# Softmax times V on one core: dropping the waits of copies and exps on their own engine's preceding write of a buffer, and one copy per loop body moved from VectorE to ScalarE

## The chip, the cores and the metric

The kernel runs on one core of one Trainium2 chip. The metric is the device time of one execution in microseconds (us).

Five engines appear below: TensorE (PE in the profile, with PEld for its weight loads), VectorE (DVE), ScalarE (ACT), GpSimd (POOL), and SyncE (SP), which issues the transfers (DMA).

## The reference

```python
def reference(scores, v):          # scores 8x12x1024x1024, v 8x12x1024x64, float32
    scores_max = np.max(scores, axis=-1, keepdims=True)
    attn = np.exp(scores - scores_max)
    attn = attn / (np.sum(attn, axis=-1, keepdims=True) + 1e-8)
    return np.matmul(attn, v).astype(np.float32)
```

There are 96 heads. The scores are 403 MB, so each element is read once and everything else has to hide behind that read.

## The kernel before

A head's 1024 query rows lie as 8 rows of 128 (one per partition). Four heads form a loop body (24 bodies), so a body has 32 such rows. One row goes through these stages:

1. ScalarE takes the exp of the scores (two rows per instruction; one at a time for the last six rows of a body).
2. PE transposes the row in eight 128x128 pieces into a PSUM tile `psT`.
3. VectorE copies `psT` to an SBUF tile `pt` (four of each, used in turn).
4. PE multiplies `pt` with V and a column of ones in eight accumulating products, two rows later.
5. After four or eight rows VectorE takes the reciprocals of the sums and scales the result; SyncE stores it.

```python
    def finish(u):                      # two rows behind
        ...
        for c in range(C):              # C = 8
            nc.tensor.matmul(
                out=bank[:, g * M : (g + 1) * M],
                lhsT=pt[:, c * P : (c + 1) * P],
                rhs=st["vones"][:, c, 0:M],
                start=(c == 0),
                stop=(c == C - 1),
            )
        if k % 2 == 1:
            if g == G - 1 and (b > 0 or k < AHEAD - 1):
                normalise(k, st, b, b + 1)
        ...
    def heads(n0):
        for k in range(AHEAD):          # 4 heads
            for r in range(R):          # 8 rows
                ...                     # exp of one or two rows into p_nat (ScalarE)
                psT = take(psT_bufs)
                for c in range(C):
                    nc.tensor.transpose(
                        out=psT[:, c * P : (c + 1) * P],
                        in_=p_row[:, c // L, c % L, :],
                        identity=order16[:],
                    )
                pt = take(pt_bufs)
                copy = nc.vector.tensor_copy(out=pt[:], in_=psT[:])
                if k == AHEAD - 1 and r == R - 1:
                    normalise(k, st, 0, 1, copy)   # first half of the last head
                ...
                if len(pending) > LAG:             # LAG = 2
                    finish(pending.pop(0))
```

Nothing in the source says so, but in the compiled program every one of PE's instructions, each weight load and each matmul, adds 1 to PE's semaphore when it is done.

The softmax here doesn't subtract the row's maximum and nothing guards it: scores larger than these inputs give would overflow.

## Time and profile before

| | before |
|---|---|
| device time, median of 3 runs | 1063.8 us (1063.76 to 1064.1) |
| span of the profiled run | 1062.3 us |
| busy: PE, PEld, DVE, ACT | 722.0, 676.5, 679.9, 740.1 us |
| DMA in use at nine tenths or more | 39 of 40 slices, about 432 GB/s |
| last row of scores lands, its exp starts | 1052.02, 1052.27 us |
| last copy on VectorE starts | 1055.18 us |
| last scaling product ends, second store issued, landed | 1058.00, 1058.25, 1060.30 us |

Times of single events are from the start of the span. The page is read from the outside in: whether one resource is full over the whole span (it is the DMA), and where it stops being full (after 1050 us, the tail). This is PE's timeline for the same steady stretch (start, duration, engine, line, instructions in the group):

```profile
26.28 0.61 PE L267 MATMUL psT<-order,p_nat 128*128 128x128 f16 x8
...
26.98 0.61 PE L267 MATMUL psT<-order,p_nat 128*128 128x128 f16 x8
...
27.69 0.61 PE L267 MATMUL psT<-order,p_nat 128*128 128x128 f16 x8
```

The transposes of successive rows start 0.70 us apart, and end, by the trace, at 26.89, 27.59 and 28.30. So by these records PE delivers a row every 0.70 us, VectorE can copy one every 0.60 us, and yet a copy comes only every 0.96 us.

### The profile page before, as it was taken

To read this page: it belongs to the slowest core of one execution; us is meant where nothing else is said; L and a number is where in the kernel's file an instruction comes from. 1 tells how busy PE (TensorE), PEld (TensorE's weight loads), DVE (VectorE), ACT (ScalarE), POOL (GpSimd) and SP (SyncE) were. 2 spreads that over 40 slices of the span, in tenths; PEclk is the share of its full clock that TensorE was granted. 3 is DMA by queue.
4 is the path that set the end of the run, shared out by engine and by line. 5 is a ranking of instruction groups with operands and counts; after the bars stand their busy time and mean duration, and the time that the engine had idled before them with its cause. 6 is when DMAs were issued, how large, how long until landed. Compare 5 with 4: busy or idle time off the path is not lost.

```text
span 1062.3 us, 33094 instructions
## 1 busy us (share of the span) xinstructions
PE 722.0 (68%) x12288; PEld 676.5 (64%) x12288; DVE 679.9 (64%) x1205; ACT 740.1 (70%) x480; POOL 243.5 (23%) x406
## 2 busy tenths in 40 slices
PE   2765766767766767667576776767677686666776
PEld 2755756666655667666576666766566676665765
DVE  1765756757666666666676666767567576676667
ACT  3766776666767668676685866767666677666686
POOL 3113112131121311212112221132121311203113
PEclk9988888879898787887988878889888788899889
DMA  9999999999999999999999999999999999999996
GB/s 397 430 417 434 428 434 434 432 435 428 434 432 432 427 433 435 434 434 427 433 429 435 428 433 435 426 441 431 431 434 429 430 428 438 434 434 432 426 432 260
DMA packets 25059, 453.05 MB, mean 426 GB/s; under 512 B 2784, under 2 KB 2784, under 8 KB 9440
## 3 DMA queue, kind: packets, MB, share of 16 engines
q1 hardware_dynamic: 25056, 453.00, 99.4%
q8 instruction: 3, 0.05, 0.0%
HBM read 436.21 MB, written 25.17 MB: 434 GB/s over the span
## 4 chain that ended last, share of the span: by engine, by line
DMA 62%; PE 12%; PEld 6%; DVE 5%; ACT 5%; issue 3%; POOL 3%; SPq 1%; POOLq 1%; ACTq 0%; DVEq 0%; PEldq 0%
DMA s_nat<-in_scores_dram 62%; PE psT L267 7%; DVE pt L273 5%; ACT p_nat L255 5%; PE psO L146 3%; POOL vones L212 3%; PEld L267 3%; PEld L146 3%; PE psO_whole L146 1%; SPq L203 1%; SPq L191 0%; POOLq L212 0%; POOLq L229 0%; POOLq L293 0%; POOLq L321 0%
## 5 line engine op out<-in xcount | busy, mean ns | idle before, releaser
L255 ACT ACTIVATE p_nat<-s_nat 128x2048 f16<-128x2048 f32 (+1 forms) x456 | 709.4, 1630 | 219.1 <-DMA s_nat<-in_scores_dram 192.3
L267 PE MATMUL psT<-order,p_nat 128*128 128x128 f16 x6144 | 562.8, 246 | 281.3 <-ACT p_nat L255 280.9
L273 DVE COPY pt<-psT 128x1024 f16<-128x1024 f16 x768 | 518.1, 689 | 367.1 <-PE L146 134.9
L267 PEld LDWEIGHTS <-p_nat 128*128 128x128 f16 x6144 | 445.4, 123 | 303.5 <-ACT p_nat L255 300.8
L212 POOL CAST vones<-v_sb 32x512 f16<-32x512 f32 x400 | 242.8, 607 | 815.3 <-PE L267 440.3
L146 PEld LDWEIGHTS <-pt 128*128 128x128 f16 x6144 | 302.8, 106 | 76.1 <-DVE pt L273 72.0
L146 PE MATMUL psO<-vones,pt 128*128 128x65 f16 x3072 | 177.5, 202 | 41.4 <-DVE pt L273 39.8
L146 PE MATMUL psO_whole<-vones,pt 128*128 128x65 f16 x3072 | 189.7, 209 | 11.6 <-DVE pt L273 11.2
L255 ACT ACT_TABLE_LOAD x24 | 30.8, 1283 | 94.1 <-DMA s_nat<-in_scores_dram 77.4
L130 DVE TENSOR_TENSOR out_sb<-psO,recip 64x256 f32<-64x256 f32 x192 | 81.2, 423 | 6.1
L130 DVE TENSOR_TENSOR out_sb<-psO_whole,recip 64x512 f32<-64x512 f32 x96 | 66.0, 688 | 3.0
L123 DVE RECIPROCAL recip<-psO 128x4 f32<-128x4 f32 x96 | 16.8, 175 | 0.8
L123 DVE RECIPROCAL recip<-psO_whole 128x8 f32<-128x8 f32 x48 | 9.5, 197 | 0.0
L71 DVE MEMSET vones<- 128x16 f16 x4 | 0.2, 72 | 0.8 <-PEq L310 0.8
L62 DVE CAST order<-ident 128x128 f16<-128x128 f32 x1 | 0.2, 227 | 0.4 <-POOL ident masks.py:199 0.4
masks.py:199 POOL TENSOR_SCALAR_AFFINE_SELECT ident<-ident 128x128 f32<-128x128 f32 x1 | 0.3, 292 | 0.1
masks.py:197 POOL MEMSET ident<- 128x128 f32 x1 | 0.2, 204 | 0.3 <-POOLq L310 0.3
L310 POOL MEMSET const-float32-0.0<- 128x1 f32 x1 | 0.1, 98 | 0.3 <-issue 0.3
L310 POOL MEMSET const-bfloat16-1.0<- 128x1 bf16 x1 | 0.1, 100 | 0.0
L310 POOL MEMSET const-uint8-127<- 128x1 uint8 x1 | 0.1, 100 | 0.0
L310 POOL MEMSET const-float32-1.0<- 128x1 f32 x1 | 0.1, 98 | 0.0
## 6 DMA issues: line engine op xcount, KB each, us to landing
s_nat<-in_scores_dram SPq DMA_DIRECT2D x96, 4096.0 KB, 33.0
v_sb<-in_v_dram SPq DMA_DIRECT2D x24, 1024.0 KB, 19.0
out_dram<-out_sb SPq DMA_DIRECT2D x47, 512.0 KB, 27.7
s_nat<-in_scores_dram SPq DMA_DIRECT2D x2, 2048.0 KB, 32.6
s_nat<-in_scores_dram SPq DMA_DIRECT2D x1, 1536.0 KB, 32.2
s_nat<-in_scores_dram SPq DMA_DIRECT2D x3, 512.0 KB, 20.7
s_nat<-in_scores_dram SPq DMA_DIRECT2D x1, 1024.0 KB, 25.4
out_dram<-out_sb SPq DMA_DIRECT2D x2, 256.0 KB, 2.0
```

The source lines that it names most:

```text
L62: nc.vector.tensor_copy(out=order16[:].rearrange("p (t j) -> p t j", t=T), in_=ident32[:].rearrange("p (j t) -> p t j", t=T),)
L71: nc.vector.memset(vo[:, :, D : D + 2], 1.0)
L123: inverse = nc.vector.reciprocal(out=recip, in_=psO[:, :, :, D : D + 1])
L130: nc.vector.tensor_tensor(out=rows.rearrange("j (b g) d -> j b g d", g=G), in0=psO[part, :, :, 0:D], in1=recip[part].to_broadcast([W, last ...
L146: nc.tensor.matmul(out=bank[:, g * M : (g + 1) * M], lhsT=pt[:, c * P : (c + 1) * P], rhs=st["vones"][:, c, 0:M], start=(c == 0), stop=(c ...
L203: nc.sync.dma_start(out=v_sb[:].rearrange("x h s l d -> x (h s l d)"), in_=rows[bass.ds(n // AHEAD, 1)].rearrange("o x y -> (o x) y"),)
L212: nc.gpsimd.tensor_copy(out=vones_bufs[k][s * Q : (s + 1) * Q, :, 0:D].rearrange("i (h l) d -> i h l d", l=L), in_=v_sb[k * Q : (k + 1) * ...
L255: nc.scalar.activation(out=p_nat[:, g : g + rows, :].rearrange("p r (x v) -> p x r v", v=Q * L), in_=s_bufs[k][:, r + g : r + g + rows, :] ...
L267: nc.tensor.transpose(out=psT[:, c * P : (c + 1) * P], in_=p_row[:, c // L, c % L, :], identity=order16[:],)
L273: copy = nc.vector.tensor_copy(out=pt[:], in_=psT[:])
L310: nc = _bacc.Bacc("TRN2", target_bir_lowering=False, num_devices=1)
```

## The change

Its intent: a copy into `pt` and an exp into `p_nat` need not wait for the earlier write of the same buffer by the same engine, since PE, which reads the buffer in between, is waited for anyway. The change declares those dependencies away. And in each body the copy of the last head's seventh row (index 6) goes to ScalarE, so that VectorE has less in front of the last copy.

```diff
     stores = []
-
-    def apart(dma, other):
-        tc.declare_no_dep(
-            dma.ins, other.ins, across_iterations=True, reason="stores of two heads are disjoint"
-        )
+    writers = {}
+
+    def apart(a, b, reason="stores of two heads are disjoint"):
+        tc.declare_no_dep(a.ins, b.ins, across_iterations=True, reason=reason)
+
+    def rewrite(buf, op):
+        others = writers.setdefault(buf.name, [])
+        for other in others:
+            apart(op, other, "readers in between")
+            apart(other, op, "readers in between")
+        apart(op, op, "readers in between")
+        others.append(op)
 ...
-                        nc.scalar.activation(
+                        exp = nc.scalar.activation(
 ...
+                        rewrite(p_nat, exp)
 ...
                 pt = take(pt_bufs)
-                copy = nc.vector.tensor_copy(out=pt[:], in_=psT[:])
+                if k == AHEAD - 1 and r == R - 2:
+                    nc.scalar.copy(out=pt[:], in_=psT[:])
+                else:
+                    copy = nc.vector.tensor_copy(out=pt[:], in_=psT[:])
+                    rewrite(pt, copy)
```

## The prediction

> **What bounds the kernel now.** I read the page's 40 slices and its DMA part first, then the chain that ended last, then the groups, and last the timeline of VectorE (DVE) in a steady stretch and at the end. The slices and the DMA part:
>
> ```profile
> DMA  9999999999999999999999999999999999999996
> GB/s 397 430 417 434 428 434 434 432 435 428 434 432 432 427 433 435 434 434 427 433 429 435 428 433 435 426 441 431 431 434 429 430 428 438 434 434 432 426 432 260
> ...
> q1 hardware_dynamic: 25056, 453.00, 99.4%
> ...
> DMA 62%; PE 12%; PEld 6%; DVE 5%; ACT 5%; issue 3%; POOL 3%; SPq 1%; POOLq 1%; ACTq 0%; DVEq 0%; PEldq 0%
> ```
>
> In 39 of 40 slices the DMA engines are at nine tenths or more, at about 432 GB/s; only the last slice falls to six tenths and 260 GB/s. The one queue's packets take 99.4% of the 16 engines' span, and the chain that ended last is led by DMA with 62%. 453.0 MB at 432 GB/s are 1049 us of the span of 1062.3. So the kernel is a transfer of 1050 us with a tail behind it. The windows put an edge on the tail (DMA share and GB/s are the last two numbers of a row):
>
> ```profile
> 148.00:1020.00 872.00, 604.05 (x10232) 567.26 (x10232) 565.42 (x997) 615.68 (x400) 194.00 (x320) 0.85 1.00 432
> ...
> 1048.00:1050.00 2.00, 2.00 (x47) 1.90 (x44) 1.46 (x3) 1.55 (x2) 0.00 (x0) 1.00 0.73 297
> 1050.00:1052.00 2.00, 2.00 (x37) 1.65 (x34) 1.78 (x5) 2.00 (x3) 1.82 (x3) 1.00 0.20 82
> 1052.00:1054.00 2.00, 1.23 (x22) 0.87 (x21) 1.97 (x4) 1.30 (x2) 0.61 (x1) 1.00 0.53 217
> 1054.00:1056.00 2.00, 1.52 (x34) 1.27 (x33) 1.81 (x5) 0.00 (x0) 0.00 (x0) 1.00 0.11 45
> 1056.00:1058.00 2.00, 0.36 (x8) 0.23 (x8) 1.87 (x5) 0.00 (x0) 1.19 (x2) 1.00 0.00 0
> ```
>
> Over 872 us the DMA share is 1.00. After 1050 it collapses, and DVE, the third engine of a row after PE and PEld, is busy 1.8 to 1.97 of every 2 us until 1058. That is the only stretch in which DVE can set the time.
>
> The groups concerned:
>
> ```profile
> L255 ACT ACTIVATE p_nat<-s_nat 128x2048 f16<-128x2048 f32 (+1 forms) x456 | 709.4, 1630 | 219.1 <-DMA s_nat<-in_scores_dram 192.3
> ...
> L273 DVE COPY pt<-psT 128x1024 f16<-128x1024 f16 x768 | 518.1, 689 | 367.1 <-PE L146 134.9
> ```
>
> DVE's 768 copies are 689 ns each; DVE idles 367 us in front of them and the page says mostly for PE. The timeline says otherwise (start, duration, idle before):
>
> ```profile
> 27.36 0.69 DVE L273 COPY pt<-psT 128x1024 f16<-128x1024 f16 x1 [0.27 <-PE L267]
> 28.32 0.69 DVE L273 COPY pt<-psT 128x1024 f16<-128x1024 f16 x1 [0.27 <-PE L146]
> 29.28 0.69 DVE L273 COPY pt<-psT 128x1024 f16<-128x1024 f16 x1 [0.27 <-PE L146]
> ...
> 1052.54 2.48 DVE L273 COPY pt<-psT 128x1024 f16<-128x1024 f16 x4
> 1055.18 0.69 DVE L273 COPY pt<-psT 128x1024 f16<-128x1024 f16 x1 [0.16 <-PE L146]
> 1055.79 0.17 DVE L123 RECIPROCAL recip<-psO 128x4 f32<-128x4 f32 x1
> 1056.00 0.88 DVE L130 TENSOR_TENSOR out_sb<-psO,recip 64x256 f32<-64x256 f32 x2
> 1056.91 0.18 DVE L123 RECIPROCAL recip<-psO 128x4 f32<-128x4 f32 x1
> 1057.12 0.88 DVE L130 TENSOR_TENSOR out_sb<-psO,recip 64x256 f32<-64x256 f32 x2
> ```
>
> In the steady stretch copies come every 0.96 us with the same gap of 0.27 us, although PE's transposes for them end earlier (those for the copy at 28.32 end at 27.59, modelled). Four copies in a row at 1052.54 overlap and come every 0.60 us. So DVE itself loses 0.36 us on some copies. I sorted all 768 copies by their place in the loop body (32 places). Each copy's loss is its start, less the later of "transposes done plus 0.04" and "DVE free". Places 5 to 7, 9, 22, 23 and 31, where DVE was the later of the two, lose 0.358 us at the median; places 12 to 14, 20, 28 and 29 lose 0.006. In the trace the first kind has a fused register operation (46 ns) and a separate wait on DVE's own semaphore (21 ns) in front of the copy, executed as the preceding copy starts. The second kind has only a single register operation, or had both done two copies ahead.
>
> **What the Trainium skill says.** "Perfetto Trace Analysis", section Identifying Dependency Chains: instructions that wait for several engines may get separate event-semaphore instructions in front. The trace agrees: those are the 21 ns records, one per copy of the first kind. "VectorE: DVE Perf Modes", section The DRAIN you can't avoid, measured that semaphores between copies cost nothing extra; this trace differs where the wait is a separate instruction, 0.96 against 0.60 us from start to start, and I follow the trace. "ScalarE: Activation LUTs", section Table sets, says copy is in every table set, so the new ScalarE copy should bring no table load beyond the 24 of now. Its section What ACT_TABLE_LOAD costs gives 186 ns + 0.833 ns per element, 1.04 us for 1024; the trace's 128x1024 exps take 1.04 us, so I take that for the copy. "DMA: Bandwidth & Descriptors", section Where 436 GB/s comes from, puts the ceiling at 435 GB/s; the trace runs at 432 to 434, so the steady part has nothing to give.
>
> **The change part by part.**
>
> DVE's own waits: 768 less 24 copies remain on DVE; each that now waits on itself should fall to the second kind. Seven to ten of 32 copies in a body lose up to 0.36 us, some 3 us per body, 24 bodies, near 70 us of DVE idle in all. All of it but the last body lies beside transfers: a transfer takes about 33 us from issue to landing at the median, and 14 us even for the quickest load, so the queue stays full whatever DVE does. On the path: nothing before 1050 us.
>
> ScalarE's own waits: exps of 2048 elements already follow each other every 1.80 us with a duration of 1.90, so they overlap and their waits are done ahead. Worth 0.
>
> The tail, instruction by instruction (single records of the trace). The last row of scores lands at 1052.02. ScalarE, busy with the rows before it, does its exp from 1052.27 to 1053.30; the change moves neither. PE could then transpose at about 1053.36, but does so only at 1054.16, because earlier work in its order waited for the copy at 1052.54, which stood behind 1.41 us of DVE normalisation of the head before. The last copy starts at 1055.18: DVE is held by the sixth-row copy (1054.35 to 1055.03), then loses the 0.36. Everything behind is serial on DVE: reciprocal, two products, reciprocal, two products, until 1058.00; the second store is issued at 1058.25 and lands at 1060.30; the end is 1062.26.
>
> With the change: DVE's arrears at 1045 to 1050 (copies at 1045.58, 1046.54, 1047.50 and 1048.52, each about 0.96 apart) go, so the normalisation of the head before is over before the exps of rows 3 to 7 come, which arrive only every 0.95 us. Copy 6 goes to ScalarE: free at about 1053.2, 1.04 us, done at 1054.25. PE transposes row 7 from 1053.36 to 1053.97 (0.61), and DVE's last copy starts 0.04 later, 1054.01 instead of 1055.18. That is 1.17 us. PE's products need the ScalarE copy at 1054.3 and the last one ends near 1055.2, before DVE wants it at about 1055.7 (1056.91 less 1.17), so the DVE series keeps its length. Sum: 0 steady, 0 at the start, 1.17 at the end. 1063.8 less 1.17 is 1062.6; I say 1062.7, since PE's order in the new program may cost a tenth.
>
> **The rivals.** First, the gain is nothing or even a small loss: the build orders each engine's instructions anew, and with fewer dependencies PE might put a product that waits for ScalarE's copy before the last transposes, which would cost back up to 0.9 us (1054.25 against 1053.36): 1063.5. For it speaks that in the present program a group of eight transposes is already split 4 and 4 around products of an earlier row; against it, that the products lag two rows. Second, the DVE idle is on the path after all, since the freed buffers let loads be issued sooner: some 3 us a body would be 70 us, so 994 us. Against it stand the DMA share of 1.00 and 432 GB/s; I give it next to nothing. Third, ScalarE becomes the bound, or delays loads: 24 copies of 1.04 us add 25 us to 740 of 1062, and they fall where ScalarE idles before the next head's landing (in the page it waits 192 us for scores). That would leave 1063.8. A table load per copy, if the page on ScalarE were wrong, would add 2 x 1.28 us a body, hidden as well except perhaps 1.3 in the tail.
>
> **Range and chances.** The tail's gain lies between 0 and about 1.3 us: it cannot exceed what the landing at 1052.02 allows, about 1.17 plus the 0.17 that ScalarE runs behind it. Executions of before lie within 0.34 us. So 1062.1 to 1063.7, centre 1062.7. A change of 2% is 21 us, more than the whole 12 us after the transfers; faster or slower by that has one chance in a hundred each.
>
> **What would show it.** In the changed profile: DMA slices and 432 GB/s as now; the 0.27 gaps before copies gone, copies 0.60 apart when PE is ahead; DVE's idle before copies with other releasers but hardly less busy time (518 us less 24 x 0.69, 501); 24 ScalarE copies near 1.04 us and still 24 table loads; the last row landing at about 1052.0 and its exp starting at 1052.1 to 1052.3; the last DVE copy near 1054.0; the span near 1061.2. I am wrong if the landing itself moves by over half a microsecond, if copies keep a pitch of 0.96 us, or if PE's last transposes start later than 1053.6.

## The result, and the profile after

| | before | after |
|---|---|---|
| device time, median of 6 runs | 1064.01 us (1063.76 to 1064.28) | 1064.35 us (1063.92 to 1064.81) |
| ratio after/before, 95% interval | | 1.0003 (0.9991 to 1.0016) |
| instructions | 33094 | 32352 |
| span of the profiled run | 1062.3 us | 1063.0 us |
| last row's exp starts | 1052.27 | 1052.22 |
| last copy on VectorE starts | 1055.18 | 1055.41 |

A ratio is the mean time of one kernel's fast runs over the mean of the other's of the same rounds, so it is not quite the ratio of the medians quoted beside it. The interval contains 1: the change is worth nothing that these runs can show. 1.1 us were predicted; the result lies outside the predicted range.

The page of the kernel after: the DMA in 40 slices, GB/s, the load queue, and the chain that ended last.

```profile
DMA  9999999999999999999999999999999999999995
GB/s 396 431 426 433 422 431 434 433 434 434 434 434 433 422 438 426 433 434 434 434 427 441 433 432 433 423 431 433 434 434 432 435 434 434 432 430 425 431 433 247
...
q1 hardware_dynamic: 25056, 453.00, 99.3%
...
DMA 62%; PE 16%; ACT 5%; PEld 4%; issue 4%; POOL 3%; DVE 3%; SPq 1%; POOLq 1%; ACTq 0%; DVEq 0%
```

DMA leads as before. VectorE's part of the chain fell from 5% to 3%, and that of PE and PEld together rose from 18% to 20%. The windows (busy time and count of PE, PEld, DVE, ACT, POOL; clock; DMA share; GB/s):

```profile
148.00:1020.00 872.00, 604.71 (x10224) 567.97 (x10224) 552.47 (x977) 635.76 (x420) 195.07 (x320) 0.84 1.01 432
...
1052.00:1054.00 2.00, 1.13 (x21) 0.82 (x18) 1.94 (x5) 1.27 (x2) 0.81 (x2) 1.00 0.51 209
1054.00:1056.00 2.00, 1.61 (x36) 1.33 (x33) 1.25 (x3) 1.01 (x1) 0.00 (x0) 1.00 0.13 53
1056.00:1058.00 2.00, 0.50 (x11) 0.31 (x8) 1.84 (x7) 0.00 (x0) 0.96 (x2) 1.00 0.04 8
```

The steady window is unchanged at 432 GB/s. From 1054 to 1056 VectorE is now busy 1.25 us where it was busy 1.81: it does less there, and still finishes no earlier. The groups:

```profile
L264 ACT ACTIVATE p_nat<-s_nat 128x2048 f16<-128x2048 f32 (+1 forms) x456 | 709.5, 1630 | 217.5 <-DMA s_nat<-in_scores_dram 187.4
...
L287 DVE COPY pt<-psT 128x1024 f16<-128x1024 f16 x744 | 502.9, 690 | 382.5 <-PE psO_whole L146 120.1
...
L285 ACT COPY pt<-psT 128x1024 f16<-128x1024 f16 x24 | 24.3, 1012 | 48.2 <-issue 45.9
L264 ACT ACT_TABLE_LOAD x24 | 30.8, 1283 | 25.3 <-SPq L308 16.8
```

Both parts of the change arrived: 24 copies are ScalarE's, 1012 ns each, with no table load more than the 24 of before. One thing was left undone: `rewrite` is called for VectorE's copies only. In the trace ScalarE's copies still wait for ScalarE's own semaphore, with a separate wait instruction for PE and VectorE in front, and 24 of VectorE's copies now wait for ScalarE. But VectorE's idle time in front of its copies did not shrink. It is 382.5 us where it was 367.1, and the page still names PE. VectorE's timeline, steady and in the tail:

```profile
26.76 0.69 DVE L287 COPY pt<-psT 128x1024 f16<-128x1024 f16 x1 [0.27 <-PE L146]
27.71 0.69 DVE L287 COPY pt<-psT 128x1024 f16<-128x1024 f16 x1 [0.27 <-PE L277]
...
1052.77 1.89 DVE L287 COPY pt<-psT 128x1024 f16<-128x1024 f16 x3
1055.41 0.69 DVE L287 COPY pt<-psT 128x1024 f16<-128x1024 f16 x1 [0.75 <-PE psO L146]
...
1057.35 0.88 DVE L130 TENSOR_TENSOR out_sb<-psO,recip 64x256 f32<-64x256 f32 x2
```

The pitch is still 0.96 us and the gap still 0.27 us, without any wait of VectorE for itself in front of a copy: the trace now shows a single register operation of 40 ns (720 for 744 copies), where before it showed the fused one of 46 ns and the wait of 21 ns. In the tail VectorE now idles 0.75 us before the last copy. ScalarE in the tail:

```profile
1048.41 4.86 ACT L264 ACTIVATE p_nat<-s_nat 128x1024 f16<-128x1024 f32 x5 [0.82 <-PE psO_whole L146]
1054.58 1.01 ACT L285 COPY pt<-psT 128x1024 f16<-128x1024 f16 x1 [1.30 <-PE L277]
```

ScalarE's last exp ends at 1053.27, and its copy starts 1.30 us later; the prediction had them back to back. It waits for PE, though the transposes it needs end, by the trace, at 1054.18.

**What PE's semaphore shows.** The trace records every addition to a semaphore, with its time; no view of the profile prints them, so the figures of this part were worked out from the trace itself. PE's semaphore gets 24,576 additions in both kernels, which is 12,288 weight loads and as many matmuls. In the kernel before, 22,649 of the gaps between two of them are 30 ns (within 1 ns), and none is shorter than 29. Setting each copy beside the addition of its last transpose gives this table (us; "end" is the end that the trace gives the transposes):

```
kernel  transposes end   addition    copy starts   engine
before       26.186        26.375       26.398     DVE
before       26.890        27.335       27.359     DVE
before       27.594        28.295       28.319     DVE
before       28.299        29.255       29.279     DVE
before     1054.767      1055.161     1055.184     DVE   (last copy)
after      1046.196      1046.749     1046.773     DVE
after      1046.900      1047.709     1047.733     DVE
after      1054.177      1054.429     1054.577     ACT
after      1054.997      1055.389     1055.412     DVE   (last copy)
```

Over all copies of either trace, none on VectorE starts less than 0.022 us after the addition. In the kernel before, 524 of the 768 start within 0.024 us of it, and the other 244 follow at once on earlier work of VectorE's. The additions lag the ends of the transposes by 0.28 us at the median and 1.23 us at most. (ScalarE's copy comes 0.148 us after the addition in the kernel after, behind its separate wait instruction, and 0.022 us after it in e6 below, where the copy itself waits for PE.) One row takes 8 weight loads and 8 matmuls for the transposes and the same again for the products: 32 additions of 30 ns, 0.96 us. That is the pitch of the copies.

In the tail the additions leave as one train. Its last gap is at 1037.941 us before and at 1038.169 after; from there to the last addition (1056.600 and 1056.829) every gap is 30 ns, and both trains last 18.66 us, 622 additions. The addition that the last copy waits for comes 17.22 us after the start of the train in both, and behind that copy VectorE works in series to the end. The train began 0.23 us later in the run after; the last copy came 0.23 us later too.

The profiled run after ends at 1063.03, not at 0.23 us past 1062.26, because its last store landed at 1061.25 after an issue that took 1.01 us (0.33 before). The other five runs of the kernel after have spans of 1061.9 to 1062.9, and 18 runs of the kernel before have 1061.9 to 1063.1, so nothing here points to the change.

### The profile page after: what moved, and what is told of

Its sections match the earlier page's. It is cut to its first block, busy times and chain, and to the rows that moved or that the text cites. A ratio compares the mean times of both kernels' runs of the same rounds, so it can differ in the third digit from the quotient of the medians.

```text
span 1063.0 us, 32352 instructions
## 1 busy us (share of the span) xinstructions
PE 722.7 (68%) x12288; PEld 677.1 (64%) x12288; DVE 664.7 (63%) x1181; ACT 764.6 (72%) x504; POOL 244.5 (23%) x406
## 4 chain that ended last, share of the span: by engine, by line
DMA 62%; PE 16%; ACT 5%; PEld 4%; issue 4%; POOL 3%; DVE 3%; SPq 1%; POOLq 1%; ACTq 0%; DVEq 0%
DMA s_nat<-in_scores_dram 62%; PE psT L277 9%; PE psO L146 6%; ACT p_nat L264 5%; POOL vones L221 3%; DVE pt L287 3%; PEld L277 3%; PE psO_whole L146 2%; PEld L146 2%; SPq L212 1%; SPq L200 0%; POOLq L221 0%; POOLq L238 0%; ACT pt L285 0%; POOLq L308 0%
## 5 line engine op out<-in xcount | busy, mean ns | idle before, releaser
L264 ACT ACTIVATE p_nat<-s_nat 128x2048 f16<-128x2048 f32 (+1 forms) x456 | 709.5, 1630 | 217.5 <-DMA s_nat<-in_scores_dram 187.4
L287 DVE COPY pt<-psT 128x1024 f16<-128x1024 f16 x744 | 502.9, 690 | 382.5 <-PE psO_whole L146 120.1
L146 PEld LDWEIGHTS <-pt 128*128 128x128 f16 x6144 | 302.4, 106 | 77.1 <-DVE pt L287 56.3
L146 PE MATMUL psO<-vones,pt 128*128 128x65 f16 x3072 | 177.9, 202 | 41.9 <-DVE pt L287 25.5
L146 PE MATMUL psO_whole<-vones,pt 128*128 128x65 f16 x3072 | 189.1, 208 | 11.9 <-DVE pt L287 11.5
L285 ACT COPY pt<-psT 128x1024 f16<-128x1024 f16 x24 | 24.3, 1012 | 48.2 <-issue 45.9
```

Source lines behind the costliest of these rows:

```text
L146: nc.tensor.matmul(out=bank[:, g * M : (g + 1) * M], lhsT=pt[:, c * P : (c + 1) * P], rhs=st["vones"][:, c, 0:M], start=(c == 0), stop=(c ...
L264: exp = nc.scalar.activation(out=p_nat[:, g : g + rows, :].rearrange("p r (x v) -> p x r v", v=Q * L), in_=s_bufs[k][:, r + g : r + g + ro ...
L285: nc.scalar.copy(out=pt[:], in_=psT[:])
```

## The experiments

Two theories. **W**, the prediction's: the separate wait of VectorE on its own semaphore costs up to 0.36 us per copy, and the change failed to make use of its removal for some other reason (the order of PE, the place of ScalarE's copy). **U**: PE's additions leave one per 30 ns, and 32 of them make the 0.96 us; VectorE's waits cost nothing. U says that the pitch follows the number of additions, whatever VectorE's program is, and that the tail's 1.17 us come only if PE adds less often.

Each of the four experiments e1 to e4 changes the number of additions and leaves VectorE's copies as they are in the kernel before, with their own waits. Experiments e5 and e6 take the two halves of the change alone. Experiments e7 and e8 put the change on top of fewer additions. e1 to e4 ran on one chip beside 9 runs of the kernel before (median 1064.0), e5 to e8 on another beside 9 (median 1064.11).

### e1_two_products: more additions

Each product is made in two column halves, 32 and 33 wide: the same products, but 24 matmuls and 24 weight loads per row where there were 16 of each, so 48 additions per row where there were 32.

```diff
-        for c in range(C):
-            nc.tensor.matmul(
-                out=bank[:, g * M : (g + 1) * M], ...
+        for m0, m1 in ((0, 32), (32, M)):
+            for c in range(C):
+                nc.tensor.matmul(
+                    out=bank[:, g * M + m0 : g * M + m1], ...
```

> The kernel before with each row's product made in two column halves (32 and 33 of 65), so that TensorE carries out 48 instructions a row instead of 32. Theory U (TensorE's semaphore updates leave one per 30 ns and pace everything): 48 x 30 ns = 1.44 us a row, 768 rows = 1106 us, more than the transfers' 1050, so the kernel becomes bound by updates: 1115 to 1140 us, slower by 5 to 7%, copies 1.44 us apart. Rival P (TensorE's work itself, or VectorE's own waits, pace the copies): TensorE's busy time a row rises from about 0.7 to about 1.0 us, still under the 1.36 us a row of the transfers: within 1% of before, copies at most 1.0 us apart.

Measured: correct, 1152.41 us (1152.14 to 1152.99, 4 runs), ratio 1.0831 (1.0815 to 1.0848). PE's line of the page, the steady window, and VectorE's steady timeline:

```profile
PE 1070.8 (93%) x18432; PEld 1051.9 (91%) x18432; DVE 699.6 (61%) x1205; ACT 742.7 (65%) x480; POOL 243.7 (21%) x406
...
148.00:1020.00 872.00, 829.02 (x14292) 814.35 (x14291) 541.96 (x931) 578.77 (x372) 181.56 (x299) 0.96 0.97 403
...
100.04 0.69 DVE L274 COPY pt<-psT 128x1024 f16<-128x1024 f16 x1 [0.75 <-PE L147]
101.48 0.69 DVE L274 COPY pt<-psT 128x1024 f16<-128x1024 f16 x1 [0.75 <-PE L147]
```

The copies come 1.44 us apart, 48 times 30 ns, with VectorE's program untouched. PE with its additions is now the bound, and the load stream falls to 403 GB/s. The expectation of the time was too low: it took 36,864 additions of 30 ns, 1106 us, and allowed too little around them. In the trace the first addition comes at 20.1 us, what the gaps between additions have beyond 30 ns sums to 19.6 us, and 5.3 us follow the last addition: 20.1 + 1105.9 + 19.6 + 5.3 = 1150.9, the span of 1150.8.

### e2_two_products_few: the same instructions, fewer additions

The rival for e1 is that PE simply needs longer for 48 instructions. So e2 runs the instructions of e1, but the program is edited after tracing: in each run of one row's transposes, or of its products, only the last matmul adds to the semaphore, and it adds the run's count. The waits are unchanged; each is met at the end of a run.

```diff
+def fewer_updates(nc):
+    ...
+        def close():
+            for i in run[:-1]:
+                i["sync_info"]["on_update"] = []
+            if run:
+                (u,) = run[-1]["sync_info"]["on_update"]
+                u.update(update_mode="sem-add-imm", update_value=len(run))
+            run.clear()
+    ...
+    nc = fewer_updates(nc)
     r = _run(nc, [arrays], core_ids=[0])
```

> As e1, the same instructions on every engine, but TensorE tells of a run (one row's transposes, or its products) once, at the run's last matmul, by the run's count. Theory U: the slowness of e1 goes, back within 1% of before (1064), copies about 1.0 us apart or less. Rival P: as e1 gives, whatever that is, since TensorE's work is unchanged.

Measured: correct, 1063.44 us (1063.38 to 1063.72, 4 runs), ratio 0.9994 (0.9979 to 1.0009). PE's line of the page, one group of matmuls, and five copies of VectorE's steady timeline:

```profile
PE 790.0 (74%) x18432; PEld 767.3 (72%) x18432; DVE 676.9 (64%) x1205; ACT 740.2 (70%) x480; POOL 243.5 (23%) x406
...
L147 PE MATMUL psO<-vones,pt 128*128 128x32 f16 (+1 forms) x6144 | 216.2, 180 | 6.7 <-DVE pt L274 4.2
...
99.56 3.32 DVE L274 COPY pt<-psT 128x1024 f16<-128x1024 f16 x5
```

All of e1's 88 us are gone with the same 18,432 matmuls, and copies can follow each other 0.66 us apart (five in 3.32 us). The rival falls. PE's busy time is 790.0 us here and 1070.8 us in e1, yet a matmul is recorded as no longer there. The same group in e1:

```profile
L147 PE MATMUL psO<-vones,pt 128*128 128x32 f16 (+1 forms) x6144 | 377.3, 177 | 25.3 <-DVE pt L274 23.4
```

One matmul took 177 ns at the mean, here 180. What differs is when matmuls start: from 200 to 1000 us in e1, 10,305 of the 13,114 gaps between two starts are 60 ns, two additions (its weight load's and its own); here 4 of 14,076 are, and the median is 27 ns. The records overlap less, so their union grows. So the additions hold up PE itself once they back up, and PE's busy time is no measure of its work then.

### e3_half_products: fewer additions in another way

Only half of each product is computed, so a row has 24 additions, and no edit of the program after tracing is involved.

```diff
-        for c in range(C):
+        for c in range(C // 2):
             ...
-                stop=(c == C - 1),
+                stop=(c == C // 2 - 1),
```

> Wrong on purpose: only 4 of the 8 chunks enter each row's product, so 24 TensorE instructions a row. Theory U: where VectorE follows TensorE's updates, copies come every 24 x 30 ns = 0.72 us instead of 0.96. Rival W (a register operation and wait in front of a copy costs VectorE 0.36 us): 0.96 us stays, since VectorE's program is the same. The time within 1.5 us of before in both, by U 0.5 to 1.2 us under it.

Measured: wrong as intended, one run of unknown state, 1062.97 us, span 1061.2.

```profile
26.46 1.29 DVE L273 COPY pt<-psT 128x1024 f16<-128x1024 f16 x2 [0.27 <-PE L267]
28.11 1.29 DVE L273 COPY pt<-psT 128x1024 f16<-128x1024 f16 x2 [0.36 <-PE L267]
```

VectorE's program is nearly the same as before (456 separate waits for itself in front of copies, 480 before), yet the copies come in pairs 0.60 us apart, two per 1.65 us, 0.82 a row. Where the additions of 24 set the pace, the pitch is 0.72 (24.78 to 25.50, and 1045.75 to 1046.47 in the tail). But such places are few, and from 1044 to 1055.2 us the additions fill only 0.73 of the time: another limit is close behind. The last copy starts at 1054.28. W, which has the pitch in VectorE's own program, can't give this.

### e4_before_few: the kernel before, one addition per run

```diff
 # the kernel before
+    nc = fewer_updates(nc)
     r = _run(nc, [arrays], core_ids=[0])
```

> The kernel before, with TensorE telling of a run once, as in e2. Theory U: the copies' pitch of 0.96 us falls to 0.60 to 0.72 us, the normalisation of the head before the last is over before 1050 us, the last VectorE copy starts at 1053.9 to 1054.7 instead of 1055.2, span 1061.0 to 1061.8 instead of 1062.3, time 0.5 to 1.3 us under before. Rival W: pitch 0.96 stays, since VectorE's own waits stay, and the time is that of before within 0.3 us.

Measured: correct, 1063.33 us (1063.04 to 1063.65, 5 runs), ratio 0.9993 (0.9980 to 1.0007), an interval that contains 1.

```profile
25.39 4.21 DVE L273 COPY pt<-psT 128x1024 f16<-128x1024 f16 x6 [0.51 <-PE psT L267]
...
1053.29 1.40 DVE L273 COPY pt<-psT 128x1024 f16<-128x1024 f16 x2 [0.52 <-PE psT L267]
...
1055.93 0.88 DVE L130 TENSOR_TENSOR out_sb<-psO,recip 64x256 f32<-64x256 f32 x2
```

With all of VectorE's own waits in place, six copies run in 4.21 us with no gap and 0.704 us apart, PE's own pitch. The second copy of the group at 1053.29 is the last one and starts at 1054.00; the prediction had computed 1054.01 for the changed kernel. The last product ends at 1056.81 instead of 1058.00. One expectation failed: the scaling of the head before ends at 1050.83, not before 1050. The mean span of the five runs is 1060.82, against 1062.21 of the nine runs before, 1.39 us less. The device time fell by 0.67 only: in this kernel time and span differ by 1.9 to 2.95 us, in the kernel before, on the same chip, by 1.7 to 2.0. What lies in that difference, no view shows; it stays open.

### e5_waits_only: the first half of the change

The change with all copies on VectorE.

```diff
-                if k == AHEAD - 1 and r == R - 2:
-                    nc.scalar.copy(out=pt[:], in_=psT[:])
-                else:
-                    copy = nc.vector.tensor_copy(out=pt[:], in_=psT[:])
-                    rewrite(pt, copy)
+                copy = nc.vector.tensor_copy(out=pt[:], in_=psT[:])
+                rewrite(pt, copy)
```

> The first part of the change alone: copies and exps without the waits for their own engine's writes, all copies on VectorE. Theory U (TensorE's updates, one per 30 ns, pace the copies): in the tail the copies stay 0.96 us apart, the last one starts at 1055.0 to 1055.4 as before, span 1062.0 to 1062.7, time within 0.4 us of before. Rival W (own waits cost VectorE 0.36 us, and the ScalarE copy takes the gain back): span 1061.0 to 1061.9, time 0.4 to 1.2 us under before.

Measured: correct, 1064.66 us (1064.05 to 1064.95, 5 runs), ratio 1.0006 (0.9992 to 1.0019).

```profile
1047.38 0.69 DVE L283 COPY pt<-psT 128x1024 f16<-128x1024 f16 x1 [0.27 <-PE L277]
...
1055.06 0.69 DVE L283 COPY pt<-psT 128x1024 f16<-128x1024 f16 x1 [0.16 <-PE L146]
```

The pitch and the gaps are those of the kernel before. The median is 0.55 us above that of the kernel before, where up to 0.4 was expected; the interval contains 1. The train of additions lasts 18.66 us again (1037.814 to 1056.473).

### e6_scalar_only: the second half of the change

The kernel before with row 6 of the last head copied by ScalarE.

```diff
-                copy = nc.vector.tensor_copy(out=pt[:], in_=psT[:])
+                if k == AHEAD - 1 and r == R - 2:
+                    nc.scalar.copy(out=pt[:], in_=psT[:])
+                else:
+                    copy = nc.vector.tensor_copy(out=pt[:], in_=psT[:])
```

> The second part alone: ScalarE makes the sixth row's copy of each fourth head, waits kept. Theory U: the last VectorE copy is released by TensorE's update for the last transposes, 0.3 to 0.5 us after their modelled end, not by VectorE's copy before it; it starts at 1055.1 to 1055.5, span 1062.0 to 1062.9, time within 0.5 us of before. Rival W: as e5 is faster, this one is slower than before by what the change showed too little, 0.7 to 1.2 us. Rival P0 (the ScalarE copy alone shortens the tail): the last copy at 1054.4 to 1054.7, 0.5 to 0.8 us under before.

Measured: correct, 1063.88 us (1063.77 to 1064.76, 5 runs), ratio 1.0 (0.9987 to 1.0014).

```profile
1055.10 0.69 DVE L276 COPY pt<-psT 128x1024 f16<-128x1024 f16 x1 [0.75 <-PE psO L146]
```

ScalarE's copy starts at 1054.14 and relieves VectorE of the copy of that row; the 0.60 us that this frees on VectorE turn into 0.75 us of idle time before the last copy. Train: 1037.861 to 1056.521, 18.66 us.

### e7_after_few: the whole change, one addition per run

```diff
 # the kernel after
+    nc = fewer_updates(nc)
     r = _run(nc, [arrays], core_ids=[0])
```

> The whole change, with TensorE telling of a run once, as in e4. Theory U: the prediction's tail comes true: ScalarE's copy runs at 1053.2 to 1054.3, the last VectorE copy starts at 1053.9 to 1054.2, span 1060.7 to 1061.3, all of it already there in e4 (last copy 1054.00, span 1060.9): time within 0.4 us of e4. If the change has a worth of its own once the updates are out of the way, it is at least 0.4 us faster than e4.

Measured: correct, 1062.83 us (1062.60 to 1063.07, 5 runs), ratio 0.9988 (0.9974 to 1.0001).

```profile
1053.64 1.01 ACT L285 COPY pt<-psT 128x1024 f16<-128x1024 f16 x1 [0.16 <-ACT p_nat L264]
...
1054.22 0.69 DVE L287 COPY pt<-psT 128x1024 f16<-128x1024 f16 x1 [1.22 <-PE psT L277]
```

ScalarE's copy now follows its last exp after 0.16 us, much as predicted, though 0.34 us later than the 1053.3 expected. The last copy on VectorE is 1.80 us after the start of the last exp (1052.42; its row had landed at 1052.24), and in e4 it is 1.80 us too (1054.00 less 1052.20). The mean spans are 1060.90 here and 1060.82 in e4 (on another chip, where the kernel before had nearly the same time). So also where the additions are out of the way the change adds nothing that the spans show: the last copy then waits for the last exp and the last transposes, and VectorE idles 1.22 us before it. By device time the expectation failed. The median here is 0.50 us under that of e4, and 0.4 was set as the sign of a worth of its own. All of it lies in e4's unexplained time outside the span, and the two ran on different chips, so whether the change has such a worth is not settled.

### e8_few_early_norm: a use for that idle time

e7, but the first half of the last head is scaled where it falls in the row order, ahead of the last copy, and no longer behind it.

```diff
-            if g == G - 1 and (b > 0 or k < AHEAD - 1):
+            if g == G - 1:
                 normalise(k, st, b, b + 1)
 ...
-                if k == AHEAD - 1 and r == R - 1:
-                    normalise(k, st, 0, 1, copy)
```

> As e7, and the first half of the last head is normalised as soon as its products are there, before the last copy and not behind it. VectorE is free there once ScalarE makes the sixth row's copy: reciprocal and two products at 1053.1 to 1054.2, last copy at 1054.1 to 1054.4, only one reciprocal and two products behind the last product. Span 1060.2 to 1060.6, 0.3 to 0.7 us under e4 and e7. If the products of row 3 arrive late, the last copy is held past 1054.6 and nothing is won.

Measured: correct, 1062.63 us (1062.51 to 1062.65, 5 runs), ratio 0.9986 (0.9972 to 0.9999).

```profile
1054.45 0.69 DVE L287 COPY pt<-psT 128x1024 f16<-128x1024 f16 x1
1055.67 0.18 DVE L123 RECIPROCAL recip<-psO 128x4 f32<-128x4 f32 x1 [0.52 <-PE psO L146]
```

The scaling now ends at 1054.43 and pushes the last copy to 1054.45, so part of the gain is given back, and VectorE then idles 0.52 us for the last products. The expectation was missed on each count, though not by much: the last copy at 1054.45 (1054.4 at the latest), the mean span 1060.72 (1060.2 to 1060.6), the time 0.2 us under e7 (0.3 to 0.7). From the start of the last exp to the end of the last product it is 4.29 us, against 4.62 in e7 and 5.73 in the kernel before. This is the fastest kernel, 1.5 us (0.14%) below the kernel before by the medians, and still "the same" by a measure of 2%.

## Why the prediction was wrong

**The step that failed** is "So DVE itself loses 0.36 us on some copies". It rested on three readings: PE's transposes had ended, VectorE was free, and a wait of VectorE on itself stood in front of just the slow copies. The first reading was the error. It took the modelled end of the transposes as the moment when VectorE could know of them. The moment that counts is the addition to PE's semaphore, and it came up to 1.23 us later. The 0.36 us is 0.96 less 0.60: 32 additions of 30 ns, less the pitch of VectorE's copies. The own wait that stood in front of the slow copies was a companion, not the cause: e4 has all of these waits and a pitch of 0.704, and the kernel after and e5 have none of them in front of copies and keep 0.96. Nor does the last copy lose 0.36, as the prediction says of it: its own line gives 0.16 us of idle time, and the copy starts 0.84 us after the one before. That one started 0.147 us behind its addition because VectorE was busy; the last one started 0.023 us behind its own.

The page had named the right engine. Its group line gives PE's L146 as the largest part of VectorE's 367.1 us of idle time (134.9), and the waits view gives PE 362.8 us in all; the prediction overruled this with "The timeline says otherwise". And it set the Trainium skill aside at the one place where it was asked: "VectorE: DVE Perf Modes", section The DRAIN you can't avoid, has the semaphores between copies cost nothing extra. e3, e4 and e5 agree with that page: in e3 copies follow each other 0.60 us apart with these waits between them.

The page that bears on the cause isn't named in the prediction, and the change touches no PE instruction. "TensorE: Matmul & The Clock Gate", section The cost: per-tile semaphore tail, says that increments on completion serialize, fits 26.3 ns to each, and calls a single one, on the last tile's matmul, sound (e2, e4, e7 and e8 gave correct results with it). An estimate from that page would have been 32 times 26.3 ns, 0.84 us per row; the trace has 0.96. "Perfetto Trace Analysis", section Summary: the profiler window per engine type, says that TensorE's end is an estimate and that the propagation of a semaphore is not in the profile; this trace agrees, with the lag of 0.28 us at the median.

The other steps, in their order:

- **The steady part gives 0: right.** The window from 148 to 1020 us stays at 432 GB/s. PE's additions fill 0.704 of the time from 200 to 1000 us in both kernels, so neither VectorE's pitch nor PE's additions matter there. e1 shows what is needed to matter: 48 additions a row.
- **ScalarE's own waits are worth 0: right.** The exps' group took 709.4 us before and 709.5 after, with 219.1 and 217.5 us of idle time in front.
- **The copy on ScalarE: right.** 1012 ns for the 1.04 us that were estimated, and no table load more, as "ScalarE: Activation LUTs", section Table sets, has it.
- **The landing and the exp of the last row: right.** 1052.06 and 1052.22, in the ranges given.
- **"DVE's arrears at 1045 to 1050 ... go": wrong**, by the same cause. Copies at 1046.77, 1047.73 and 1048.75 were still waiting for additions. With them the rest of the tail fell: ScalarE's copy at 1054.58 for "about 1053.2", the last transposes at 1054.39 for 1053.36, the last copy at 1055.41 for 1054.01.
- **The size of the gain, 1.17 us, was right for another kernel, and that is luck as far as the change goes.** It is what PE's additions cost at the last copy: e4 starts it at 1054.00, 1.18 us earlier than before, with nothing of the change in it.

Of the rivals, the first and the third named an outcome near the real one (1063.5 and 1063.8) by causes that did not occur: PE's order splits the eight transposes 4 and 4 in both kernels, and ScalarE is no bound. That the change would do nothing because PE's signals are the limit was not among them.

**The range was too narrow for what the text itself listed.** Two of three rivals left the time about where it was, yet the range ended at 1063.7, below the median of the kernel before. A range that held the outcome "nothing happens" with the usual scatter would have gone to about 1064.3 (the slowest of the six runs of the kernel before took 1064.28), and the median of the kernel after, 1064.35, lies at that edge. The limit of the gain was also loose: it counts 0.17 us from the landing to the exp where the prediction's own times, 1052.02 and 1052.27, give 0.25. The chances in the classes of 2% were right.

The marks that the prediction set for itself did their work: "if copies keep a pitch of 0.96 us, or if PE's last transposes start later than 1053.6". Both occurred.

What stays open: why the train of additions begins at 1037.81 to 1038.17 in these runs (the exps before it start within 0.08 us of each other in the traces of before and after, so this is only part of the 0.23); the device time of e4 outside the span, and with it whether the change is worth something once the additions are fewer; and whether the 30 ns belong to this one semaphore, to PE, or to the way between them, since no run used a second semaphore.

## What to carry to other kernels

Before you charge an idle gap to the engine that idles, compare its start with the arrival of the signal that it waits for, not with the recorded end of the producer's work. A producer with many short instructions, each of which signals, can be limited by its signals: count the signals per unit of work, multiply by the smallest gap between them, and see whether it gives the pitch. And a pitch that is an exact multiple of such a gap, the same to the hundredth in place after place as here (32 times 30 ns, then 48 times), is a reason to test this before you blame a wait in the consumer.

## What the Trainium skill lacked or had wrong

- "TensorE: Matmul & The Clock Gate", section The cost: per-tile semaphore tail, has the mechanism for packed tiles, with 26.3 ns per increment. These traces show 30 ns between additions of ordinary 128-row matmuls (22,649 of the gaps in the kernel before).
- The same section speaks of MATMULs. Here the weight loads' additions count in the same way: 32 per row, 16 of them of weight loads, make the pitch of 0.96 us. It also gives the cost as a tail behind one group; here it goes on as a backlog over 19 rows, 622 additions without a gap in 18.66 us.
- "Perfetto Trace Analysis", section Identifying the Most-Contended Engine, calls matmul busy time a bad measure because pipelined instructions look smaller. No page says that a backlog of additions also makes busy time larger, by spreading the starts of records that are no longer than before: 1070.8 us in e1 for the matmuls that fill 790.0 us in e2; PEld's busy time, which the section recommends instead, went the same way, 1051.9 against 767.3.
- "ScalarE: Activation LUTs", section What ACT_TABLE_LOAD costs: its formula gives 1.04 us for 1024 elements; ScalarE's copy from PSUM to SBUF took 1.012 us.
